# Up-projections as seven block products in 18 of 22 units of a two-layer encoder step

## The chip, the cores and the metric

One core of a Trainium2 chip. The metric is the device time of one execution in microseconds, the median of the runs shown. The engines are named as in the profile: PE (TensorE, matmuls), PEld (its weight loads), DVE (VectorE), ACT (ScalarE), POOL (GpSimd), SP (SyncE, which here only issues DMAs). Each engine works through its own queue of instructions in order; an instruction that waits holds up all that stand behind it on that engine.

## What is computed

The reference is one inference step of a two-layer trunk on 640 tokens: 512 of a new prompt and 16 next tokens of each of 8 running streams. Layer 0 has a mixer of gated spatial and convolutional heads, layer 1 a forgetting attention; each is followed by a channel mixer, the part that the change is about:

```python
def _conv_ffn(x, prev, w_up, conv_w, w_down):
    z, st = _causal_dwconv(x @ w_up, conv_w, prev)
    gate, up = jnp.split(z, 2, axis=-1)
    return (jax.nn.silu(gate) * up) @ w_down, st
```

Its input is the RMS-normed residual, d_model is 1024, d_ff is 2816, so `w_up` is 1024 x 5632 and `w_down` 2816 x 1024. All is float32. The last two rows of `x @ w_up` of each sequence are returned as new state.

## The kernel before

Tokens lie along the free axis, features on partitions. d_model is 8 chunks of 128 (`NC`), d_ff is 22 units of 128 (`NJ`), and a unit is a gate block and an up block (44 blocks, `NB`).

A float32 product is made of three float32r matmuls (`mm`): weight high times operand high, weight high times operand low, weight low times operand high. Each runs over 320 of the 640 tokens (`HT`), so one 128 x 128 piece of a weight costs six matmuls. The two halves of the tokens meet at a bank border of one PSUM tile.

Weights come from DRAM as float32 by a DMA that SP issues (`weights`); ACT casts them to the high part `whi` (L88) and DVE subtracts that from the raw tile to get the low part `wlo` (L89). The pool `wts` has three buffers of each of raw, high and low. The operands, residual times the norm's gain, are made in `prep` (ACT's `hh` L131, DVE's `hl` L132); the norm's root, one factor per token, is spread over partitions as `rb` and multiplied in when a block leaves PSUM. ACT squares the residual (L138) and POOL sums the squares (L139) for the next norm.

`ffn` treats the units in parts of 6, 6, 5 and 5. `up(j)` loads the two blocks' weights, runs 2 x 48 matmuls (`blocks`, L109), evacuates each block into a padded tile `zp` (L190 prompt, L191 streams, DVE), saves the new state (L202, POOL), convolves (one ACT product L196, two DVE taps L198 a block), applies silu to the gate (L355, ACT), multiplies gate and up (L358 and L359, DVE) and splits the product into high and low (ACT L97, DVE L98). After each part `project` runs the down-projection of that part, eight blocks, each added to the residual (L209); the next part's first unit is computed ahead of it. In the last part of layer 0 `prep` of the next norm follows each block.

The instructions of each engine are put into an order when the program is built, which need not be the order of the code: what the tables of rows below show is what stands in each engine's queue.

Of the kernel before, what the change touches and what calls it, by code (L numbers as in the profile page):

```python
# [8 lines left out]
F32 = mybir.dt.float32  # L9
# [34 lines left out]
# columns of the constants of the attention  # L44
# [4 lines left out]
NS = 256 + 16      # keys of a stream  # L49


class Core:
    def __init__(self, ctx, tc, io):
# [16 lines left out]
        self.n = 0  # L70

# [4 lines left out]
    # ---- weights: float32 from DRAM, split exactly into two float32r parts  # L76
    def weights(self, src, cols=1024, pieces=1, between=None):
        nc = self.nc
        raw = self.wp.tile([P, 1024], F32, tag="raw", name=self.nm("raw"))
# [12 lines left out]
    def split(self, pool, tags, src):  # L92
        """float32 [128, 640] -> (hi, lo) float32r tiles"""
        nc = self.nc
        hi = pool.tile([P, T], F32R, tag=tags[0], name=self.nm("sh"))
        lo = pool.tile([P, T], F32R, tag=tags[1], name=self.nm("sl"))
        nc.scalar.copy(out=hi, in_=src)  # L97
        nc.vector.tensor_tensor(out=lo, in0=src, in1=hi.bitcast(F32), op=ALU.subtract)  # L98
        return hi, lo

    # ---- products, weights stationary, tokens moving
# [10 lines left out]
    def psum(self):  # L112
        return self.pm.tile([P, 1024], F32, tag="mm", name=self.nm("mm"))
# [11 lines left out]
    # ---- RMS norm: operands scaled by g now, by the root later  # L125
# [28 lines left out]
    def stats(self, acc, pool, aux):  # L154
        """1/rms for each token, as columns [128, 5]"""
# [8 lines left out]
    def spread(self, rt, pool, aux):  # L164
        """columns [128, 5] -> the same along the free axis of every partition"""
# [727 lines left out]
```

## Time and profile before

| | |
|---|---|
| runs, us | 1533.40, 1533.43, 1536.4; median 1533.43 |
| span of the profiled execution, us | 1531.9 |
| first mixer, us from the start of the span | 0 to 227 |
| channel mixer of layer 0 | 227 to 680 |
| attention with its projections | 680 to 1076 |
| channel mixer of layer 1 | 1076 to 1523 |
| bytes moved by DMA | 142.90 MB, mean 93 GB/s |

The profiled execution's own time is its span and the little that lies around it, so that a sum of durations is made against 1531.9 us and then brought to the median of the runs. In the rows of the profile, "L109" is line 109 of the kernel; `out<-in` names tiles; after "x" stands the number of instructions; then busy time in all, mean ns of one, and the idle time of that engine ahead of them with what ended it. In rows of a timeline the first numbers are the start and the duration. In rows that group instructions by line, three numbers with slashes are the shortest, the median and the longest duration in ns. In rows by window the engines stand in the order PE, PEld, DVE, ACT, POOL, then the granted clock, the DMA share and GB/s.

### The profile page before, as it was taken

How to read it: one execution, taken by the hardware profiler on the slowest of the kernel's cores; microseconds unless marked ns; L12 is line 12 of the kernel's file. 1: busy time of each engine (PE TensorE's matmuls, PEld its weight loads, DVE VectorE, ACT ScalarE, POOL GpSimd, SP SyncE). 2: the span in 40 equal slices, each digit the busy share in tenths (PEclk: the TensorE clock that was granted, in tenths of full speed). 3: DMA queues.
4: the chain of work that ended last, by engine and by line, in shares of the span. 5: the costliest groups of instructions: out<-in, count | busy, mean ns of one | idle time of the engine just before them, and what ended most of it. 6: DMA issues, size and time to landing. Idle time of an engine off the chain costs nothing.

```text
span 1531.9 us, 26648 instructions
## 1 busy us (share of the span) xinstructions
PE 1517.8 (99%) x11008; PEld 1473.5 (96%) x11008; DVE 899.1 (59%) x1541; ACT 559.4 (37%) x918; POOL 237.4 (15%) x281
## 2 busy tenths in 40 slices
PE   8999999999999999999999999999999999999999
PEld 6999999999999999999989888888999999999998
DVE  6545437644653655675676766768765466365463
ACT  5422334322322322345545454535432233133231
POOL 5000122201210201143111111003221021021010
PEclk9999999999999999999999999999999999999999
DMA  6222212222223222243544343523222222321313
GB/s 226 77 82 73 77 56 85 68 81 85 62 64 95 64 66 93 62 156 103 180 128 136 122 123 104 183 60 107 83 60 76 87 67 57 98 73 53 107 47 106
DMA packets 52296, 142.90 MB, mean 93 GB/s; under 512 B 6656, under 2 KB 13744, under 8 KB 52048
## 3 DMA queue, kind: packets, MB, share of 16 engines
q1 hardware_dynamic: 45424, 133.79, 28.6%
q10 hardware_dynamic: 6752, 7.41, 1.4%
q8 instruction: 87, 1.43, 0.4%
q14 instruction: 33, 0.27, 0.1%
HBM read 125.41 MB, written 11.54 MB: 89 GB/s over the span
## 4 chain that ended last, share of the span: by engine, by line
PE 96%; DVE 2%; issue 1%; ACT 1%; DMA 0%; POOL 0%; SPq 0%; DVEq 0%; ACTq 0%
PE mm L109 71%; PE pj L507 10%; PE pv L583 3%; PE po L109 2%; PE pt L576 1%; PE mm L239 1%; PE pt L662 1%; PE sc L569 1%; DVE hl L132 1%; PE sc L570 1%; DVE wlo L89 1%; PE scs L641 1%; PE pt L537 1%; PE pt L655 0%; PE scs L634 0%
## 5 line engine op out<-in xcount | busy, mean ns | idle before, releaser
L88 ACT CAST whi<-raw 128x1024 fp32r<-128x1024 f32 (+4 forms) x222 | 207.6, 937 | 494.6 <-PE mm L109 426.1
L109 PE MATMUL mm<-hl,whi 128*128 128x320 f32 x1664 | 379.4, 309 | 0.5 <-DVE hl L132 0.5
L109 PE MATMUL mm<-hh,whi 128*128 128x320 f32 x1664 | 379.8, 309 | 0.0
L109 PE MATMUL mm<-hh,wlo 128*128 128x320 f32 x1664 | 379.2, 309 | 0.0
L109 PEld LDWEIGHTS mm<-hl,whi 128*128 128x128 f32 x1664 | 278.2, 188 | 0.7 <-DVE hl L132 0.7
L109 PEld LDWEIGHTS mm<-hh,whi 128*128 128x128 f32 x1664 | 278.2, 188 | 0.1
L109 PEld LDWEIGHTS mm<-hh,wlo 128*128 128x128 f32 x1664 | 278.0, 188 | 0.0
L89 DVE TENSOR_TENSOR wlo<-raw,whi 128x1024 fp32r<-128x1024 f32 (+4 forms) x222 | 245.5, 1107 | 33.3 <-ACT whi L88 33.0
L109 PE MATMUL mm<-sh,wlo 128*128 128x320 f32 x866 | 197.2, 309 | 1.3 <-DVE wlo L89 1.3
L109 PE MATMUL mm<-sl,whi 128*128 128x320 f32 x866 | 197.2, 309 | 0.0
L109 PE MATMUL mm<-sh,whi 128*128 128x320 f32 x866 | 196.2, 309 | 0.0
L202 POOL COPY so<-zp 128x18 f32<-128x18 f32 x88 | 89.4, 1016 | 570.4 <-DVE zp L191 570.4
L190 DVE TENSOR_TENSOR zp<-mm,rb 128x512 f32<-128x512 f32 x88 | 60.9, 692 | 195.8 <-PE mm L109 195.8
L209 DVE TENSOR_TENSOR x<-mm,x 128x640 f32<-128x640 f32 x79 | 65.0, 823 | 185.6 <-PE mm L109 185.6
L198 DVE SCALAR_TENSOR_TENSOR t<-zp,cst,t 128x656 f32<-128x656 f32 x184 | 165.1, 900 | 10.3 <-ACT t L196 5.6
L109 PEld LDWEIGHTS mm<-sh,wlo 128*128 128x128 f32 x866 | 144.6, 188 | 1.6 <-DVE wlo L89 1.6
L109 PEld LDWEIGHTS mm<-sl,whi 128*128 128x128 f32 x866 | 144.8, 188 | 0.0
L109 PEld LDWEIGHTS mm<-sh,whi 128*128 128x128 f32 x866 | 144.4, 188 | 0.2 <-issue 0.2
L507 PE MATMUL pj<-wlo,hh 128*128 128x256 f32 x480 | 137.7, 287 | 0.7 <-DVE wlo L89 0.7
L507 PE MATMUL pj<-whi,hh 128*128 128x256 f32 x480 | 137.7, 287 | 0.0
L507 PE MATMUL pj<-whi,hl 128*128 128x256 f32 x480 | 137.5, 287 | 0.0
L507 PEld LDWEIGHTS pj<-wlo,hh 128*128 128x128 f32 x480 | 91.6, 191 | 2.8 <-issue 1.6
(188 smaller groups left out, 1691.3 us busy)
## 6 DMA issues: line engine op xcount, KB each, us to landing
raw<-w_up SPq DMA_DIRECT2D x88, 512.0 KB
raw<-w_dn SPq DMA_DIRECT2D x32, 384.0 KB
raw<-w_c SPq DMA_DIRECT2D x24, 512.0 KB
raw<-w_dn SPq DMA_DIRECT2D x32, 320.0 KB
raw<-w_ab SPq DMA_DIRECT2D x16, 512.0 KB
ck<-c_k SPq DMA_DIRECT2D x16, 512.0 KB
cv<-c_v SPq DMA_DIRECT2D x16, 512.0 KB
o_kv<-z ACTq DMA_DIRECT2D x8, 640.0 KB
```

The lines of the kernel that those rows point to most:

```text
L88: nc.scalar.copy(out=hi[:, c], in_=raw[:, c])
L89: nc.vector.tensor_tensor(out=lo[:, c], in0=raw[:, c], in1=hi[:, c].bitcast(F32), op=ALU.subtract)
L109: nc.tensor.matmul(outs[h], lhsT=l, rhs=r[:, h * HT:(h + 1) * HT], start=start and k == 0, stop=stop and k == 2)
L132: nc.vector.scalar_tensor_tensor(out=lo, in0=x, scalar=gs, in1=hi.bitcast(F32), op0=ALU.mult, op1=ALU.subtract)
L190: nc.vector.tensor_tensor(out=op, in0=a[:, 0:TP], in1=b[:, 0:TP], op=ALU.mult)
L198: nc.vector.scalar_tensor_tensor(out=cv[:, 0:CW], in0=zp[:, i:i + CW], scalar=w[:, i:i + 1], in1=cv[:, 0:CW], op0=ALU.mult, op1=ALU.add)
L202: self.nc.gpsimd.tensor_copy(out=out.rearrange("p (s c) -> p s c", c=2), in_=zp[:, 496:ZW].rearrange("p (s c) -> p s c", c=18)[:, :, 16:18])
L209: self.nc.vector.tensor_tensor(out=x, in0=ps[:, C0:C0 + T], in1=x, op=ALU.add)
L239: nc.tensor.matmul(pvs[tb], lhsT=l[:, tb * P:(tb + 1) * P], rhs=r[:, (kc % 2) * 512:(kc % 2 + 1) * 512], start=kc == 0 and k == 0, stop=kc ...
L507: nc.tensor.matmul(out[tb], lhsT=l[:, tb * P:(tb + 1) * P], rhs=r[:, c:c + 256], start=kc == 0 and i == 0, stop=kc == 7 and i == 2)
L537: nc.tensor.transpose(t[:, tb * P:(tb + 1) * P], z[i][:, tb, pair * P:(pair + 1) * P], k.ident)
L583: nc.tensor.matmul(ov[64 * hh:64 * hh + 64, i * P:n], lhsT=z[2][:, j, (2 * pair + hh) * 64:(2 * pair + hh) * 64 + 64], rhs=u[:, j * P:(j + ...
```

## The change

In each channel mixer units 0 to 3 stay full products (`NSTD`); units 4 to 21 are computed by seven block products in the manner of Strassen and Winograd. The 2 x 2 blocks on the weights' side are (gate, up) by (even chunks, odd chunks) of d_model, and on the operands' side (even, odd chunks) by (first, second 320 tokens). A block product (`product`) is 4 chunks x 3 matmuls of 320 columns, so a unit takes 7 x 12 = 84 matmuls where it took 96.

The operand side is the same for all units. `forms(p)` makes it for chunk pair p behind each of the four full units: two DVE products of residual, gain and `rb` (640 columns), four sums or differences of 320 columns, of which three lie side by side in a raw tile, and a split of those 960 columns (ACT cast, DVE subtraction). `settle` splits the two 640-column operands into the tiles that held `hh` and `hl`, ahead of unit 4.

The weight side is made per unit (`pair_weights`): two raw tiles, four in-place sums of 512 columns on DVE, and splits of 1024, 512, 1024 and 1024 columns on ACT and DVE. `pair_blocks` runs the seven products, with ACT taking three intermediate sums out of PSUM (`snap`) and DVE and ACT writing the padded tiles; the norm's root is in the operands already. Two blocks of the down-projection of the previous part (four units) stand between the products. Their weights (`weights_down`) come two blocks to a tile; the low part is a negated copy of the high one by ACT, to which a DMA issued by GpSimd adds the weights from DRAM. Units 2 and 3 get their weights in that way as well (`weights_added`), unit 1 by `weights`. Convolutions are as before, the up block's first. Parts are now five of 4 units and one of 2; only the last one's down-projection is run by `project`. New states are copied by ACT. The host lays out the rows of `w_up` with the even chunks first (`KORD`). The pool `wts` has five buffers of high and low and four of raw; the scratch tiles in the channel mixers are 4 (9 before), the padded tiles 3 (4 before). PSUM has the same room as before, in two tiles `zx` and one `d`.

```diff
-PARTS = ((0, 6), (6, 12), (12, 17), (17, 22))
+PARTS = ((0, 4), (4, 8), (8, 12), (12, 16), (16, 20), (20, 22))
+NSTD = 4
+KORD = (0, 2, 4, 6, 1, 3, 5, 7)
...
-        self.wp = pool(ctx, "wts", bufs=3)
+        self.wp = pool(ctx, "wts", bufs=5)
...
+    def raw(self):
+        return self.wp.tile([P, 1024], F32, tag="raw", name=self.nm("raw"), bufs=4)
...
+    def added(self, pool, tags, raw, src, n, cols):
+        nc = self.nc
+        hi, lo = (pool.tile([P, n], F32R, tag=t, name=self.nm(t)) for t in tags)
+        nc.scalar.copy(out=hi[:, 0:cols], in_=raw)
+        nc.scalar.mul(out=lo[:, 0:cols], in_=hi[:, 0:cols].bitcast(F32), mul=-1.0)
+        nc.gpsimd.dma_start(out=lo[:, 0:cols], in_=src, accum_op=ALU.add)
+        return hi, lo
+    def weights_added(self, src):
+        raw = self.raw()
+        self.nc.sync.dma_start(out=raw, in_=src)
+        return self.added(self.wp, ("whi", "wlo"), raw, src, 1024, 1024)
...
+    def part(self, hi, lo, src):
+        nc = self.nc
         nc.scalar.copy(out=hi, in_=src)
         nc.vector.tensor_tensor(out=lo, in0=src, in1=hi.bitcast(F32), op=ALU.subtract)
...
+    def forms(self, p, x, g, rb, ring, fb):
+        nc = self.nc
+        pool, tags = ring
+        ys = [pool.tile([P, T], F32, tag=t, name=self.nm("y")) for t in tags]
+        tt, stt = nc.vector.tensor_tensor, nc.vector.scalar_tensor_tensor
+        for c, y in zip((2 * p, 2 * p + 1), ys):
+            stt(out=y, in0=x[c], scalar=self.gv[:, 8 * g + c:8 * g + c + 1], in1=rb, op0=ALU.mult, op1=ALU.mult)
+        (a1, b1), (a2, b2) = ((y[:, 0:HT], y[:, HT:T]) for y in ys)
+        t = self.raw()[:, 0:3 * HT]
+        t2, t3, t4 = (t[:, i * HT:(i + 1) * HT] for i in range(3))
+        tt(out=t3, in0=b2, in1=b1, op=ALU.subtract)
+        tt(out=b1, in0=a1, in1=b1, op=ALU.subtract)
+        stt(out=t2, in0=b2, scalar=-1.0, in1=b1, op0=ALU.mult, op1=ALU.subtract)
+        stt(out=t4, in0=t2, scalar=-1.0, in1=a2, op0=ALU.mult, op1=ALU.subtract)
+        return ys, self.split(fb, ("fbh", "fbl"), t, 3 * HT)
+    def settle(self, p, h, form):
+        ys, fb = form
+        for y, (hi, lo) in zip(ys, h):
+            self.part(hi, lo, y)
+        pick = lambda t, i: (t[0][:, i * HT:(i + 1) * HT], t[1][:, i * HT:(i + 1) * HT])
+        return dict(y1a=pick(h[0], 0), t1=pick(h[0], 1), y2a=pick(h[1], 0), y2b=pick(h[1], 1),
+                    t2=pick(fb, 0), t3=pick(fb, 1), t4=pick(fb, 2))
+    def pair_weights(self, gate, up):
+        nc = self.nc
+        H = 512
+        g, u = self.raw(), self.raw()
+        nc.sync.dma_start(out=g, in_=gate)
+        nc.sync.dma_start(out=u, in_=up)
+        w = ("whi", "wlo")
+        (g1, g2), (u1, u2) = ((t[:, 0:H], t[:, H:2 * H]) for t in (g, u))
+        add = lambda out, a, b: nc.vector.tensor_tensor(out=out, in0=a, in1=b, op=ALU.add)
+        A = self.split(self.wp, w, g, 1024)
+        yield
+        D = self.split(self.fd, ("dh", "dl"), u2, H)
+        add(u2, u1, u2)
+        add(u1, u1, g1)
+        B = self.split(self.wp, w, u, 1024)
+        add(g1, u2, g1)
+        add(g2, g2, g1)
+        C = self.split(self.wp, w, g, 1024)
+        pick = lambda t, i: (t[0][:, i * H:(i + 1) * H], t[1][:, i * H:(i + 1) * H])
+        yield dict(x11=pick(A, 0), x12=pick(A, 1), s3=pick(B, 0), s1=pick(B, 1), s2=pick(C, 0), s4=pick(C, 1), x22=D)
+    def product(self, out, w, f, name, start):
+        nc = self.nc
+        wh, wl = w
+        for p in range(4):
+            yh, yl = f[p][name]
+            c = slice(p * P, (p + 1) * P)
+            for i, (l, r) in enumerate(((wh, yh), (wh, yl), (wl, yh))):
+                nc.tensor.matmul(out, lhsT=l[:, c], rhs=r, start=start and p == 0 and i == 0,
+                                 stop=p == 3 and i == 2, skip_group_check=True)
+    def pair_blocks(self, w, f, zg, zu, states, downs):
+        nc = self.nc
+        zx = self.pz.tile([P, 1024], F32, tag="zx", name=self.nm("zx"))
+        Z, X = zx[:, C0:512], zx[:, 512:512 + HT]
+        Y = self.aux()[:, 0:HT]
+        n = TP - HT
+        str_ = lambda z: z[:, 514:ZW].rearrange("p (s c) -> p s c", c=18)
+        v = lambda t: t[:, n:HT].rearrange("p (s c) -> p s c", c=16)
+        def snap(b, mul):
+            t = self.fx.tile([P, HT], F32, tag="sn", name=self.nm("sn"), bufs=3)
+            nc.scalar.mul(out=t, in_=b, mul=mul)
+            return t
+        for z, st in zip((zg, zu), states):
+            nc.gpsimd.tensor_copy(out=str_(z)[:, :, 0:2], in_=st.rearrange("p (s c) -> p s c", c=2))
+        self.product(X, w["x11"], f, "y1a", True)
+        p1 = snap(X, 1.0)
+        self.product(Z, w["x12"], f, "y2a", True)
+        nc.vector.tensor_tensor(out=zg[:, 2:2 + HT], in0=Z, in1=p1, op=ALU.add)
+        self.product(Y, w["s3"], f, "t3", True)
+        p7 = snap(Y, -1.0)
+        self.product(X, w["s2"], f, "t2", False)
+        u = snap(X, -1.0)
+        if downs:
+            downs.pop(0)()
+        self.product(X, w["s1"], f, "t1", False)
+        nc.vector.tensor_tensor(out=zu[:, 2 + HT:514], in0=p7[:, 0:n], in1=X[:, 0:n], op=ALU.subtract)
+        nc.vector.tensor_tensor(out=str_(zu)[:, :, 2:18], in0=v(p7), in1=v(X), op=ALU.subtract)
+        self.product(Y, w["x22"], f, "t4", False)
+        nc.vector.tensor_tensor(out=zu[:, 2:2 + HT], in0=u, in1=Y, op=ALU.subtract)
+        if downs:
+            downs.pop(0)()
+        self.product(X, w["s4"], f, "y2b", False)
+        nc.scalar.copy(out=zg[:, 2 + HT:514], in_=X[:, 0:n])
+        nc.scalar.copy(out=str_(zg)[:, :, 2:18], in_=v(X))
+        while downs:
+            downs.pop(0)()
...
+        self.turn = (self.turn + 1) % 3
+        return self.psum_z() if self.turn < 2 else self.psum_d()
...
+        def down(n, acts, ob, w):
+            a, b = PARTS[n]
+            ps = self.psum_d()
+            for kc in range(b - a):
+                self.mm((ps[:, C0:512], ps[:, 512:512 + HT]), w, kc, acts[kc], kc == 0, kc == b - a - 1)
+            self.add_x(x[ob], ps)
+        def downs(n, acts, ob):
+            a, b = PARTS[n]
+            w = self.weights_down(io["w_dn"][l, ob:ob + 2][:, :, a * P:b * P], (b - a) * P)
+            return [lambda i=i: down(n, acts, ob + i, w[i]) for i in range(2)]
+        forms, f, prev = [], None, None
+        hk = [h[c] for c in KORD]
+        first = [KORD.index(c) for c in range(NC)]
+        zi = 0
+        for n, (a, b) in enumerate(PARTS):
+            si = self.fx.tile([P, 2, 64], F32, tag="si", name=self.nm("si"), bufs=2)
+            so = self.fx.tile([P, 2, 72], F32, tag="so", name=self.nm("so"), bufs=2)
+            nc.scalar.dma_start(out=si[:, :, 0:16 * (b - a)], in_=two(io["st_f"][l], NB)[:, :, 16 * a:16 * b])
+            acts, left = [], [0, 2, 4, 6] if n else []
+            for j in range(a, b):
+                zg, zu = self.zp[zi % 3], self.zp[(zi + 1) % 3]
+                zi += 2
+                sts = [si[:, i, 16 * (j - a):16 * (j - a) + 16] for i in range(2)]
+                if j < NSTD:
+                    blocks = (j, NJ + j)
+                    if j == 0:
+                        ps = self.blocks([self.weights(io["w_up"][l, i]) for i in blocks], hk, first)
+                    else:
+                        weights = self.weights if j == 1 else self.weights_added
+                        ps = [self.blocks([weights(io["w_up"][l, i])], hk)[0] for i in blocks]
+                    for z, p_, st in zip((zg, zu), ps, sts):
+                        self.pad_evac(z, p_[:, C0:C0 + T], rb, st)
                 else:
+                    w = self.pair_weights(io["w_up"][l, j], io["w_up"][l, NJ + j])
+                    next(w)
+                    dn = downs(n - 1, prev, left.pop(0))
+                    w = next(w)
+                    if f is None:
+                        f = [self.settle(p, (h[2 * p], h[2 * p + 1]), forms[p]) for p in range(4)]
+                    self.pair_blocks(w, f, zg, zu, sts, dn)
+                for i, z in enumerate((zg, zu)):
+                    self.new_state(z, so[:, i, 18 * (j - a):18 * (j - a) + 18])
+                acts.append(act(zg, zu, j))
+                if j < NSTD:
+                    forms.append(self.forms(j, x, g, rb, ring, fb))
+            for ob in left:
+                for d in downs(n - 1, prev, ob):
+                    d()
+            nc.scalar.dma_start(out=two(io["o_sf"][l], NB)[:, :, 18 * a:18 * b], in_=so[:, :, 0:18 * (b - a)])
+            prev = acts
+        self.project([io["w_dn"][l, ob][:, a * P:b * P] for ob in range(8)], prev, None, x, finish, cols=(b - a) * P, out=out)
```

Three places show what stands in the queues. In the rows a number behind a name is the tile's own, so one that returns is the same tile.

First, ACT's queue in layer 0 from the end of the first mixer to the end of unit 0. Before (`whi_2131` and `whi_2137` are the weights of unit 1, `whi_2265` the gate's of unit 2; `t_2110` and `t_2119` are unit 0's convolutions, `sh_2126` its product):

```order
L88 CAST whi_2131<-raw_2130 128x1024
L131 ACTIVATE hh_1956<-x_81,gv 128x640
L138 ACTIVATE t_1960<-x_81 128x640
L175 COPY rb_1973<-aux_1980 128x512
L176 COPY rb_1973<-aux_1981 128x128
L88 CAST whi_2137<-raw_2136 128x1024
L88 CAST whi_2265<-raw_2264 128x1024
L196 ACTIVATE t_2110<-zp_88,cst 128x656
L196 ACTIVATE t_2119<-zp_90,cst 128x656
L355 ACT_TABLE_LOAD
L355 ACTIVATE t_2110<-t_2110 128x656
L88 CAST whi_2271<-raw_2270 128x1024
```

After (`so_2004` are the new states, `t_2124` and `t_2128` unit 0's convolutions, `sh_2136` its product, `raw_2144` the sums of the forms; `whi_2154` and `whi_2209` are the weights of unit 1):

```order
L352 COPY so_2004<-zp_88 128x18
L352 COPY so_2004<-zp_89 128x18
L346 ACTIVATE t_2124<-zp_89,cst 128x656
L346 ACTIVATE t_2128<-zp_88,cst 128x656
L495 ACT_TABLE_LOAD
L495 ACTIVATE t_2128<-t_2128 128x656
L135 CAST sh_2136<-t_2133 128x640
L135 CAST sh_2149<-raw_2144 128x960
L94 CAST whi_2154<-raw_2153 128x1024
L94 CAST whi_2209<-raw_2208 128x1024
```

The casts of unit 1's weights stood ahead of unit 0's convolutions and now stand behind its product and its forms. The same rows follow units 1 and 2, with two negated copies behind the casts.

Second, PE's queue at the same place, the end of unit 0 and the start of unit 1. Before:

```order
L109 MATMUL mm_2009<-hh_1956,whi_2003 128x320 x2
L109 MATMUL mm_2009<-hl_1957,whi_2003 128x320 x2
L109 MATMUL mm_2009<-hh_1956,wlo_2004 128x320 x2
L109 MATMUL mm_2142<-hh_1572,whi_2131 128x320 x2
L109 MATMUL mm_2142<-hl_1573,whi_2131 128x320 x2
L109 MATMUL mm_2142<-hh_1572,wlo_2132 128x320 x2
L109 MATMUL mm_2142<-hh_1578,whi_2131 128x320 x2
```

After (`mm_2018` and `mm_2019` are unit 0's two blocks, `mm_2159` and `mm_2214` unit 1's):

```order
L251 MATMUL mm_2018<-hh_1957,wlo_2008 128x320 x2
L251 MATMUL mm_2019<-hh_1957,whi_2013 128x320 x2
L251 MATMUL mm_2019<-hl_1958,whi_2013 128x320 x2
L251 MATMUL mm_2019<-hh_1957,wlo_2014 128x320 x2
L251 MATMUL mm_2159<-hh_1573,whi_2154 128x320 x2
L251 MATMUL mm_2159<-hl_1574,whi_2154 128x320 x2
L251 MATMUL mm_2214<-hh_1573,whi_2209 128x320 x2
L251 MATMUL mm_2214<-hl_1574,whi_2209 128x320 x2
L251 MATMUL mm_2159<-hh_1573,wlo_2155 128x320 x2
L251 MATMUL mm_2159<-hh_1642,whi_2154 128x320 x2
```

In both, unit 1 follows unit 0 directly and nothing else stands between; the first matmul of unit 1 needs `whi_2154`, the fifth row needs `wlo_2155`.

Third, DVE's queue at the start of unit 4 in layer 0. Before (`wlo_2540` is unit 4's up weight, `wlo_2668` unit 5's gate weight; the evacuation of `mm_2459` is that of unit 3's up block):

```order
L89 TENSOR_TENSOR wlo_2540<-raw_2538,whi_2539 128x1024
L198 SCALAR_TENSOR_TENSOR t_2512<-zp_89,cst,t_2512 128x656 x2
L190 TENSOR_TENSOR zp_91<-mm_2459,rb_1973 128x512
L191 TENSOR_TENSOR zp_91<-mm_2459,rb_1973 128x8x16
L89 TENSOR_TENSOR wlo_2668<-raw_2666,whi_2667 128x1024
L198 SCALAR_TENSOR_TENSOR t_2521<-zp_91,cst,t_2521 128x656 x2
L358 TENSOR_TENSOR t_2525<-t_2512,t_2521 128x512
L359 TENSOR_TENSOR t_2525<-t_2512,t_2521 128x128
L98 TENSOR_TENSOR sl_2529<-t_2525,sh_2528 128x640
```

After (`raw_2589` holds the sums of the last forms, `hl_1895` is a settled operand, `raw_2602` and `raw_2603` the gate and up weights of unit 4):

```order
L158 SCALAR_TENSOR_TENSOR raw_2589<-y_2586,y_2585 128x320
L136 TENSOR_TENSOR hl_1895<-y_2585,hh_1894 128x640
L159 SCALAR_TENSOR_TENSOR raw_2589<-raw_2589,y_2586 128x320
L136 TENSOR_TENSOR sl_2607<-raw_2602,sh_2606 128x1024
L136 TENSOR_TENSOR sl_2595<-raw_2589,sh_2594 128x960
L136 TENSOR_TENSOR sl_2618<-raw_2603,sh_2617 128x512
L180 TENSOR_TENSOR raw_2603<-raw_2603 128x512
L180 TENSOR_TENSOR raw_2603<-raw_2603,raw_2602 128x512
L180 TENSOR_TENSOR raw_2602<-raw_2603,raw_2602 128x512
L180 TENSOR_TENSOR raw_2602<-raw_2602 128x512
L136 TENSOR_TENSOR sl_2624<-raw_2603,sh_2623 128x1024
L136 TENSOR_TENSOR sl_2630<-raw_2602,sh_2629 128x1024
```

Unit 4's weights were split ahead of unit 3's convolutions; now their splits and sums stand behind unit 3's forms and the settled operands.

More of the change, by code (lines that the diff above doesn't have):

```diff
@@ new lines, in weights_added, with weights_down @@
+    def weights_added(self, src):
+        raw = self.raw()
+        self.nc.sync.dma_start(out=raw, in_=src)
+        return self.added(self.wp, ("whi", "wlo"), raw, src, 1024, 1024)
+    def weights_down(self, src, n):
+        raw = self.raw()
+        hi, lo = (self.wp.tile([P, 1024], F32R, tag=t, name=self.nm(t)) for t in ("whi", "wlo"))
+        nc, m = self.nc, 2 * n
+        src = src.rearrange("o p c -> p o c")
+        two = lambda t: t[:, 0:m].rearrange("p (o c) -> p o c", o=2)
+        nc.sync.dma_start(out=two(raw), in_=src)
+        nc.scalar.copy(out=hi[:, 0:m], in_=raw[:, 0:m])
+        nc.scalar.mul(out=lo[:, 0:m], in_=hi[:, 0:m].bitcast(F32), mul=-1.0)
+        nc.gpsimd.dma_start(out=two(lo), in_=src, accum_op=ALU.add)
+        return [(hi[:, i * n:(i + 1) * n], lo[:, i * n:(i + 1) * n]) for i in range(2)]
@@ L166, in spread @@
         nc = self.nc
-        rb = pool.tile([P, T], F32, tag="rb", name=self.nm("rb"))
+        rb = pool.tile([P, T], F32, tag="acc", name=self.nm("rb"))
         dg = self.tmp()
@@ L201, in new_state @@
     def new_state(self, zp, out):
[L202 to L203 removed]
+        self.nc.scalar.copy(out=out.rearrange("p (s c) -> p s c", c=2),
+                            in_=zp[:, 496:ZW].rearrange("p (s c) -> p s c", c=18)[:, :, 16:18])
     def conv_compact(self, cv):
@@ new lines, in ffn, with act @@
+        two = lambda a, n: a.rearrange("p (u c) -> p u c", u=2)
+        def act(zg, zu, b):
+            cvs = []
+            for z, i in ((zu, 1), (zg, 0)):
+                o = O_CF + (l * NB + b + i * NJ) * 3
+                cv = self.conv(z, self.cst[:, o:o + 3])
+                if i == 0:
+                    nc.scalar.activation(out=cv[:, 0:CW], in_=cv[:, 0:CW], func=AF.Silu)
+                cvs.append(self.conv_compact(cv))
+            pr = self.tmp()
+            nc.vector.tensor_tensor(out=pr[:, 0:TP], in0=cvs[1][0], in1=cvs[0][0], op=ALU.mult)
+            nc.vector.tensor_tensor(out=pr[:, TP:T].rearrange("p (s c) -> p s c", c=16), in0=cvs[1][1], in1=cvs[0][1], op=ALU.mult)
+            return self.split(rpool, rtags, pr[:, :T])
```

94 lines of the change are left out of this document (36 added, 58 removed).

## The prediction

> **What bounds the kernel now.** I read the page's head and its chain by engine first, then what TensorE (PE) waits for, then the chain piece by piece.
>
> ```profile
> span 1531.9 us, 26648 instructions
> PE 1517.8 (99%) x11008; PEld 1473.5 (96%) x11008; DVE 899.1 (59%) x1541; ACT 559.4 (37%) x918; POOL 237.4 (15%) x281
> PE 96%; DVE 2%; issue 1%; ACT 1%; DMA 0%; POOL 0%; SPq 0%; DVEq 0%; ACTq 0%
> PE mm L239 <- ACT hh L131: 5.7, 1, 5.7
> PE mm L239 <- DVE wlo L89: 1.6, 1, 1.6
> PE mm L109 <- DVE wlo L89: 1.3, 1, 1.3
> ...
> 227.19 452.76 PE mm L109 x3087
> ...
> 1076.18 447.33 PE mm L109 x3050
> ```
>
> PE is busy 99% of the span. The third row says that 96% of the chain that ended last is PE. The waits (total, times, longest) are small and single, nearly all in the first 40 us. The two channel mixers are the last rows: 452.76 and 447.33 us without one break. So every matmul taken out there is worth its whole time, 452.76 / 3087 = 0.1467 us, as long as PE stays fed; and every microsecond in which it isn't fed is lost in full.
>
> ```profile
> 227.00:676.00 449.00, 449.00 (x3064) 449.00 (x3063) 259.63 (x353) 149.47 (x178) 71.22 (x89) 1.00 0.27 81
> ```
>
> Over layer 0's channel mixer VectorE (DVE, third busy time) works 259.63 of 449 us, ScalarE (ACT) 149.47, at a granted clock of 1.00. The helpers have room on average, so the question is where they stand in their queues when PE needs them.
>
> **What is taken out.** Up-projections of a layer: before 44 blocks x 8 chunks x 6 matmuls = 2112; after 4 units x 2 x 48 + 18 units x 84 = 1896. That is 216 fewer a layer, 432 in all: 432 x 0.1467 = **-63.4 us**. The down-projections have as many matmuls as before. This gain pays for 63.4 / 8 = 7.9 us at each of the eight hand-overs considered next (behind each full unit, four in each layer).
>
> **The hand-overs.** Before, the weight casts of the next units stand in ACT's queue ahead of the activation work of the unit just finished, and the waits above show that PE never stood there. After the change ACT's queue has the next unit's two casts behind all of it: state copies, convolutions, silu, product cast and the cast of the 960 operand columns. These wait on a DVE chain that starts with the unit's last matmul. PE has nothing else queued but the next unit, so the length of that chain is PE's idle time. Durations:
>
> ```profile
> L198 DVE SCALAR_TENSOR_TENSOR t<-zp,cst,t 128x656 f32<-128x656 f32 x88 | 78.9, 900 | 3.7 <-ACT t L196 1.5
> L89 DVE TENSOR_TENSOR wlo<-raw,whi 128x1024 fp32r<-128x1024 f32 x41 | 50.0, 1219 | 0.0
> L190 DVE TENSOR_TENSOR zp<-mm,rb 128x512 f32<-128x512 f32 x42 | 29.1, 692 | 95.5 <-PE mm L109 95.5
> L209 DVE TENSOR_TENSOR x<-mm,x 128x640 f32<-128x640 f32 x31 | 25.5, 823 | 70.9 <-PE mm L109 70.9
> L98 DVE TENSOR_TENSOR sl<-t,sh 128x640 fp32r<-128x640 f32 x22 | 18.1, 825 | 16.7 <-ACT sh L97 16.7
> L358 DVE TENSOR_TENSOR t<-t,t 128x512 f32<-128x512 f32 x22 | 15.3, 693 | 0.8
> L191 DVE TENSOR_TENSOR zp<-mm,rb 128x128 f32<-128x128 f32 x42 | 11.8, 282 | 0.0
> L359 DVE TENSOR_TENSOR t<-t,t 128x128 f32<-128x128 f32 x22 | 6.3, 285 | 0.0
> L88 ACT CAST whi<-raw 128x1024 fp32r<-128x1024 f32 x41 | 43.1, 1052 | 101.3 <-PE mm L109 98.0 <-issue 3.3
> L196 ACT ACTIVATE t<-zp,cst 128x656 f32<-128x656 f32 x42 | 35.5, 846 | 13.9 <-DVE zp L191 13.9
> L355 ACT ACTIVATE t<-t 128x656 f32<-128x656 f32 x22 | 16.6, 752 | 43.8 <-DVE t L198 43.8
> L97 ACT CAST sh<-t 128x640 fp32r<-128x640 f32 x22 | 16.0, 727 | 60.4 <-DVE t L359 60.4
> 227.48 0.27 ACT L176 COPY rb<-aux 128x128 f32<-128x128 f32 x1
> 232.50 3.33 DVE L198 SCALAR_TENSOR_TENSOR t<-zp,cst,t 128x656 f32<-128x656 f32 x4
> L774 DVE TENSOR_TENSOR x<-po,x x16: 473/491/492, 969.4 to 1031.1; 128x320 f32<-128x320 f32 x16
> ```
>
> *Behind unit 0*, from its last matmul on (0.2 us for its end to be seen): evacuation 0.61 + 0.28 (the rows' 0.69 and 0.28, overlapping a little) to 1.1; a state copy, priced by the 128-column copy's 0.27, to 1.4; convolution on ACT 0.85 to 2.2; four taps 3.33 to 5.5; silu 0.75 to 6.3; two products, 0.9 since they overlap, to 7.2. Then the forms: two 640-column operands and the split's subtraction (nearest row L98, 0.82; together 2.5, overlapping) and four of 320 columns (2.1, nearest row L774's 0.49) to 11.9. Then ACT's 960-column cast 1.0 to 12.9 and the two weight casts 1.05 each to 14.9. PE does 4 matmuls (0.6 us) in between, so it stands **14.3 us**. Weight lows, which only follow the casts, cost little more.
>
> *Behind units 1 and 2* the same chain, and then ACT's negated copies to 15.9 and an accumulating DMA for the lows, while PE gets through 8 matmuls: 14.7 us and the DMA's time L from issue to landing. No row shows such a transfer. Nearest rows:
>
> ```profile
> 0.00:18.00 18.00, 10.75 (x36) 8.33 (x36) 11.53 (x9) 14.65 (x21) 9.28 (x14) 1.00 0.88 335
> 2.58 4.82 DMA x<-xT
> ```
>
> 512 KB at the 335 GB/s of the first 18 us is 1.57 us, the low bound; a 320 KB load of x took 4.82 us in that crowd, scaled to 512 KB 7.7, the high bound. I take 4 between them, because the queues are nearly empty here (DMA share 0.27) but the landing has a fixed part. So 18.7 us each. The Trainium skill, "DMA: Bandwidth & Descriptors", section on the anatomy of one DMA, gives a GpSimd-issued transfer about 2.0 us plus its bytes at 436 GB/s, 3.2 us here; by that, an estimate, the sum would be 3 us lower.
>
> *Behind unit 3* DVE has eight subtractions of settled operands mixed into the chain, then the first pair unit's splits and sums: evacuation to 1.7, taps to 6.1, products 7.8, forms and subtractions to 13.8, then five splits (1.2, 1.1, 0.7, 1.2, 1.2) around four sums of 0.69, to 21.9. PE takes its first products at 16.5, 18.9 and 22.2, with 40 matmuls (5.9 us) in between: 22.2 - 5.9 = **16.3 us**.
>
> A layer: 14.3 + 2 x 18.7 + 16.3 = 68; two layers: **+136 us**.
>
> **The pair units.** One has 84 + 48 matmuls = 19.4 us of PE. DVE: splits 3 x 1.22 + 0.69, sums 4 x 0.69, taps 4 x 0.9, evacuations about 1.6, products 0.98, split 0.83, two residual additions 1.65: 16.0 us. ACT, by its rows, about 11.6. Neither is the bound, but the unit has two tight places: the second weight tile's cast waits for a slot that the previous unit's last down block frees, and the third product needs its low part soon after. The row of a cast (1.05) and a subtraction (1.22) against the PE work that stands there leave 0.35 to 0.5 us uncovered. I take 0.5 x 36 units = **+18 us**, bounds 0 and 1.5 each (0 to 54).
>
> **The tail and the clock.** The last part, two units deep, has 12 matmuls (1.76 us) a block, and in layer 0 the norm's preparation behind each block goes through a POOL addition:
>
> ```profile
> L132 DVE SCALAR_TENSOR_TENSOR hl<-x,gv,hh x32: 873/884/2210, 5.7 to 1067.4; 128x640 fp32r<-128x640 f32 x32
> L139 POOL TENSOR_TENSOR acc<-acc,t x28: 1572/1829/2536, 9.0 to 1066.3; 128x640 f32<-128x640 f32 x28
> ```
>
> POOL's 1.83 us is longer than 1.76, and DVE's 0.88 next to it stretches to 2.21: **+5 us**, 0 to 10.
>
> New here are long pauses of PE. The only one that the trace shows is the program's start:
>
> ```profile
> 10.11 0.61 PE L239 MATMUL mm<-whi,hh 128*128 128x512 f32 x1
> 10.54 0.41 PE L239 MATMUL mm<-whi,hl 128*128 128x512 f32 x1
> 10.79 0.40 PE L239 MATMUL mm<-wlo,hh 128*128 128x512 f32 x1
> 11.03 0.40 PE L239 MATMUL aux<-whi,hl 128*128 128x512 f32 x1
> ```
>
> The first matmul took 0.43 us to the next start, later ones 0.25 and 0.24: at most 0.4 us for each of eight pauses, **+3 us**.
>
> **Sum**: 1531.9 - 63.4 + 136 + 18 + 5 + 3 = 1630.5 us of span. The runs shown (1533.4 to 1536.4, median 1533.4) lie 1.5 us above the profiled span, so **1632 us**.
>
> **Rivals.** *Pair units bound by hand-offs.* If DVE's 16.0 us stretch beside POOL and the casts, as the 0.88 of L132 stretched to 2.21, each unit loses 1.5 to 2 us instead of 0.5: 1632 - 18 + 54 to 72 = 1668 to 1686. For: three engines hand one tile on within a product of 1.76 us. Against: DVE has 3.4 us of room. Chance 0.14.
>
> *Slow accumulating transfers.* With L of 8 to 12 us, four hand-overs cost 16 to 32 more: 1648 to 1664. For: they read and write, and start on POOL, whose queue is in order. Against: the load row's 7.7 was taken in a crowd of DMA share 0.88. Chance 0.08.
>
> *A clock that comes back slowly.* If the start's first pace, 0.43 us where 0.245 follows, lasted through the first 16 matmuls behind each pause (a third of a block), that would cost 8 x 16 x 0.1467 x 0.185 / 0.245 = 14 us: 1632 - 3 + 14 = 1643. For: no pause of PE in this trace is as long as those to come. Against: the start's slow pace holds for one matmul only, and PE had stood 10 us. Chance 0.08. The Trainium skill, "TensorE: Matmul & The Clock Gate", Part 1, puts TensorE at half clock after about 3.4 us without work, until it has worked about as long, and so speaks against a change that makes PE pause; by it, an estimate, eight pauses cost about 8 x 1.7 = 14 us too.
>
> *Faster: the hand-overs stay covered.* If the next unit's casts do get ahead of the forms' chain, as they did before the change, the 136 us go, and with them the clock's 3: 1632 - 139 = 1493. It decides at 7.9 us a hand-over, less the pair units' and the tail's 23 / 8 = 2.9, so at about 5 us. For: the whole of the trace, where PE waits for nothing at this place. Against: the order of ACT's queue, where the casts stand last, and no engine passes an instruction that waits. Chance 0.06, of which 0.01 ends within 0.2% of before.
>
> **How the numbers follow.** Forecast 0.64, the rivals 0.14, 0.08, 0.08 and 0.06. The lower end takes every unknown low: no hand-off losses (-18), L 1.57 (-10), no tail and no clock (-8), half a microsecond less at each of eight stops (-4): 1592. The upper takes 1.5 us a pair unit (+36) and L 7.7 (+15): 1683, rounded to 1685 for the tail. About 0.2% (3 us) is what a measurement of this kernel can tell from no change. Faster 0.05, within 0.2% 0.01, slower 0.94.
>
> **What the profile will show.** If right: eight stretches of 14 to 19 us without PE, behind units 0 to 3 of each layer, released by ACT's weight casts, by DVE's lows or by the DMA into wlo; 432 fewer 320-column matmuls at 0.147 us; a pair unit each 19.9 us; accumulating transfers that land in about 4 us; DVE under 85% in the pair units. Wrong if those stretches are under 5 us, if PE waits between the products of every pair unit for more than 1 us in all, if the transfers take over 8 us, or if matmuls behind a pause run at twice 0.147 us for microseconds.

## The result and the profile after

| | median, us | lowest to highest | ratio to before |
|---|---|---|---|
| before | 1533.5 | 1533.4 to 1536.4 | |
| after | 1644.0 | 1642.5 to 1646.3 | 1.0717 [1.0702, 1.0733] |

The changed kernel is 110 us slower, near the forecast of 1632 and inside its range. It came there by the hand-overs that the prediction put first, and by two other terms that were both wrong, in opposite directions; that these two nearly cancel is luck.

The head of the page, the row of the granted clock over 40 slices and the chain by engine:

```profile
span 1642.6 us, 26334 instructions
PE 1485.1 (90%) x10576; PEld 1431.1 (87%) x10576; DVE 1055.4 (64%) x1805; ACT 740.1 (45%) x1326; POOL 207.8 (13%) x235
PEclk9999986779999999999999999998767999999999
PE 86%; DVE 7%; DMA 2%; ACT 2%; issue 2%; POOL 0%; SPq 0%; DVEq 0%; ACTq 0%; POOLq 0%
```

PE has 432 instructions fewer (11008 before) and is busy 90% of the span instead of 99%. The clock row has two dents, at the start of each channel mixer; before it had none. What PE waited for (total, times, longest):

```profile
PE mm L251 <- ACT whi L102: 54.1, 4, 13.5
PE mm L251 <- ACT whi L94: 27.1, 2, 13.5
PE mm L251 <- DMA wlo<-w_up: 26.2, 4, 7.7
PE zx L201 <- ACT sh L135: 25.8, 2, 12.9
...
PE pj L690 <- DVE hl L282: 3.1, 4, 1.4
PE mm L251 <- DMA wlo<-w_dn: 2.0, 1, 2.0
PE zx L201 <- DVE sl L136: 1.6, 2, 0.8
```

These are the eight hand-overs: six first casts of a full unit's weights, four landings of accumulating transfers, two first casts of a pair unit. With the two small rows at the end they come to 54.1 + 27.1 + 26.2 + 25.8 + 2.0 + 1.6 = 136.8 us. Before, no row of this kind existed in the channel mixers. The pause behind unit 0 of layer 0, the first and the last of the forms on DVE, and then ACT (start, duration):

```profile
236.11 0.88 DVE L152 SCALAR_TENSOR_TENSOR y<-x,gv,rb 128x640 f32<-128x640 f32 x1
...
240.22 0.49 DVE L159 SCALAR_TENSOR_TENSOR raw<-raw,y 128x320 f32<-128x320 f32 x1
```

```profile
236.23 0.72 ACT L135 CAST sh<-t 128x640 fp32r<-128x640 f32 x1 [0.96 <-DVE t L499]
240.75 0.99 ACT L135 CAST sh<-raw 128x960 fp32r<-128x960 f32 x1 [3.79 <-DVE raw L159]
241.64 1.99 ACT L94 CAST whi<-raw 128x1024 fp32r<-128x1024 f32 x2
```

ACT stands idle 3.79 us for the last of the forms, although the weights behind it in its queue landed long before (SP issues no weight transfer between 205 and 242.96 us). PE on the other side of it:

```profile
228.75 0.46 PE L251 MATMUL mm<-hh,wlo 128*128 128x320 f32 x2
242.74 0.90 PE L251 MATMUL mm<-hh,whi 128*128 128x320 f32 x2 [13.53 <-ACT whi L94]
243.44 0.73 PE L251 MATMUL mm<-hl,whi 128*128 128x320 f32 x2
243.97 0.73 PE L251 MATMUL mm<-hh,whi 128*128 128x320 f32 x2
...
248.24 0.53 PE L251 MATMUL mm<-hh,wlo 128*128 128x320 f32 x2
248.60 0.46 PE L251 MATMUL mm<-hh,whi 128*128 128x320 f32 x2
```

The second thing to see is the pace behind the pause: pairs start 0.53 us apart (0.267 a matmul) until 248.2, and 0.29 or 0.30 (0.147) from 248.60 on. The start of this unit runs at little more than half pace for 5.5 us. In the pair units there is nothing of either. The first row is the window of unit 1, the second one of pair units (window, PE, PEld, DVE, ACT, POOL, granted clock, DMA share, GB/s):

```profile
242.80:259.70 16.90, 16.82 (x96) 16.56 (x96) 3.33 (x6) 1.04 (x2) 0.00 (x0) 0.83 0.20 63
...
445.00:710.00 265.00, 264.96 (x1808) 264.70 (x1808) 195.67 (x282) 140.89 (x230) 27.32 (x39) 1.00 0.43 105
```

Unit 1, 96 matmuls, takes 16.9 us at a mean granted clock of 0.83 where 14.1 would do. From 445 to 710 us PE is busy all through at 1.00, with DVE at 74%.

### The profile page after: what moved, and what is told of

Read it like the earlier page. It is cut to its first block, busy times and chain, and to the rows that moved or that the text cites. A ratio compares the mean times of both kernels' runs of the same rounds, so it can differ in the third digit from the quotient of the medians.

```text
span 1642.6 us, 26334 instructions
## 1 busy us (share of the span) xinstructions
PE 1485.1 (90%) x10576; PEld 1431.1 (87%) x10576; DVE 1055.4 (64%) x1805; ACT 740.1 (45%) x1326; POOL 207.8 (13%) x235
## 4 chain that ended last, share of the span: by engine, by line
PE 86%; DVE 7%; DMA 2%; ACT 2%; issue 2%; POOL 0%; SPq 0%; DVEq 0%; ACTq 0%; POOLq 0%
PE mm L251 36%; PE zx L201 19%; PE pj L690 10%; PE aux L201 8%; PE po L251 2%; PE pv L766 2%; DMA wlo<-w_up 2%; DVE t L348 2%; PE pt L759 1%; DVE hl L282 1%; PE mm L389 1%; DVE wlo L95 1%; PE pt L845 1%; PE sc L752 1%; DVE y L152 1%
## 5 line engine op out<-in xcount | busy, mean ns | idle before, releaser
L135 ACT CAST sh<-raw 128x1024 fp32r<-128x1024 f32 (+2 forms) x152 | 142.4, 944 | 204.5 <-PE zx L201 101.9
L201 PE MATMUL zx<-hh,sh 128*128 128x320 f32 x576 | 179.9, 312 | 25.8 <-ACT sh L135 25.8
L251 PE MATMUL mm<-hh,whi 128*128 128x320 f32 x512 | 125.6, 328 | 81.2 <-ACT whi L102 54.1
L136 DVE TENSOR_TENSOR sl<-raw,sh 128x1024 fp32r<-128x1024 f32 (+2 forms) x152 | 164.8, 1092 | 38.9 <-ACT sh L135 32.7
L201 PE MATMUL zx<-hh,sl 128*128 128x320 f32 x576 | 179.0, 312 | 1.6 <-DVE sl L136 1.6
L201 PE MATMUL zx<-hl,sh 128*128 128x320 f32 x576 | 179.5, 312 | 0.0
L251 PEld LDWEIGHTS mm<-hh,whi 128*128 128x128 f32 x512 | 91.9, 202 | 82.9 <-ACT whi L102 55.2
L251 PE MATMUL mm<-hh,wlo 128*128 128x320 f32 x512 | 120.5, 319 | 26.2 <-DMA wlo<-w_up 26.2
L201 PEld LDWEIGHTS zx<-hh,sh 128*128 128x128 f32 x576 | 109.9, 191 | 26.3 <-ACT sh L135 26.3
L251 PE MATMUL mm<-hl,whi 128*128 128x320 f32 x512 | 123.5, 324 | 0.3 <-DVE hl L282 0.3
```

Source lines behind the costliest of these rows:

```text
L201: nc.tensor.matmul(out, lhsT=l[:, c], rhs=r, start=start and p == 0 and i == 0, stop=p == 3 and i == 2, skip_group_check=True)
L251: nc.tensor.matmul(outs[h], lhsT=l, rhs=r[:, h * HT:(h + 1) * HT], start=start and k == 0, stop=stop and k == 2)
```

## The experiments

The theory: the next unit's casts stand behind the forms' chain on ACT, PE has nothing else, and each such pause costs a second time because the matmuls behind it run slowly. The rivals stand with each run. Ratios are to the kernel before, in runs on the same chip.

**Where the accumulating transfer goes: plain_lows.**

```diff
-                        weights = self.weights if j == 1 else self.weights_added
+                        weights = self.weights
```

> Units 2 and 3 get the low part of their weights by DVE's subtraction, as unit 1 does, in place of the accumulating transfer; nothing else changes. Theory (casts stand behind the forms' chain, and the transfer's landing adds to the pause): in the changed kernel PE waited 26.2 us for those four transfers, and each ended in a second slow start. Both go: 1644 - 26 - 4 = 1614 us, 1609 to 1620; the first part of all eight pauses stays at 13.5 us. Rival (DVE is as late as the transfer, the wait only changes its name): over 1634 us, with waits of 5 us or more for DVE's lows.

Measured: 1613.8 us, 1.0526 [1.0510, 1.0542], 30 less than the changed kernel. The waits at the hand-overs are now of one kind, for casts:

```profile
PE mm L251 <- ACT whi L94: 81.2, 6, 13.5
PE zx L201 <- ACT sh L135: 25.8, 2, 12.9
```

The casts' waits are the same to the tenth (54.1 + 27.1 before), and those for the transfer are gone. DVE's subtraction follows the casts closely enough to show no wait. The transfer itself, in the changed kernel, from issue to landing (L104, 8 transfers):

```profile
DMA to landing us min/median/max: 5.7/7.9/9.4
```

**Whether the pause slows what follows: busy_pauses.** On top of plain_lows:

```diff
                         self.pad_evac(z, p_[:, C0:C0 + T], rb, st)
+                    fill = self.aux()[:, 0:HT]
+                    for _ in range(22):
+                        nc.tensor.matmul(fill, lhsT=self.ones, rhs=zu[:, 2:2 + HT], start=True, stop=True)
```

> The kernel with plain lows, and 22 matmuls of 320 columns in plain float32 added behind each full unit, whose result nobody reads: they need the evacuated block, so they run in the pause, and PE works while it waits for the casts. Theory (a pause lets the granted clock fall, and the matmuls behind it run at 0.267 us for some 5 us): the pauses stay as long, the matmuls behind them run at 0.147 us from the first, and the time is about 8 x 2.5 = 20 us under that of the kernel with plain lows, near 1595 us, although it does more work. Rival (the slow start comes of ACT and DVE working beside PE, or of the operands): no gain against plain lows, near 1615 us, first matmuls still at 0.267 us.

Measured: 1599.6 us, 1.0434 [1.0419, 1.0450], 14 us under plain_lows by the medians, 18.5 by the profiled spans (1615.8 and 1597.3). The clock row of its page, and the same place in its timeline:

```profile
PEclk9999999999999999999999999999999999999999
```

```profile
229.92 12.08 PE L539 MATMUL aux<-zp,ones 128*128 128x320 f32 x44 [0.88 <-DVE zp L340]
242.58 0.56 PE L251 MATMUL mm<-hh,whi 128*128 128x320 f32 x2 [0.57 <-ACT whi L94]
242.98 0.46 PE L251 MATMUL mm<-hl,whi 128*128 128x320 f32 x2
```

The unit starts at the same moment as in the changed kernel (242.58 against 242.74), and now at full pace, with the clock at 1.00 from end to end. PE does 8 x 12.1 us of work that nobody needs, and the kernel is faster. ACT and DVE do the same beside it as in plain_lows, so they aren't what slowed the matmuls; PE's own idleness is.

**Whether it is the forms that hold the casts: forms_ahead.**

```diff
+                    forms.append(self.forms(j, x, g, rb, ring, fb))
                     for z, p_, st in zip((zg, zu), ps, sts):
                         self.pad_evac(z, p_[:, C0:C0 + T], rb, st)
...
-                if j < NSTD:
-                    forms.append(self.forms(j, x, g, rb, ring, fb))
```

> The forms of each full unit, which need nothing of that unit's result, are issued ahead of its evacuation; the same instructions. Theory (the casts wait because they stand behind the forms): the next unit's casts now stand behind the convolutions at most. By the rows, pauses of about 5.5, 3, 10.5 (the transfer's landing) and 5 us in a layer where 69 us were: 1644 - 90 - 12 for the clock = 1542 us, 1525 to 1560. Rival (the chain of evacuation, taps, silu and product holds the casts as well, the forms are only its last 5.7 us): 8 x 5.7 = 46 us less, 1595 us or more.

Measured: 1542.3 us, 1.0053 [1.0032, 1.0075]. The rival's 1595 is far off. The waits:

```profile
PE mm L251 <- DMA wlo<-w_up: 26.1, 4, 9.5
PE mm L251 <- ACT whi L94: 8.9, 2, 4.4
PE mm L251 <- ACT sh L135: 6.1, 3, 3.1
```

One instruction sequence moved in the queues takes 102 us off. Behind unit 0 there are 4.4 us left for the convolutions, where 5.5 were forecast; the transfers' landing stays, since their negated copies still stand behind convolutions.

**What is left if the weights go ahead too: both_ahead.** On top of forms_ahead:

```diff
+                    if j + 1 < NSTD:
+                        ws = load(j + 1)
+                    else:
+                        pw = self.pair_weights(io["w_up"][l, NSTD], io["w_up"][l, NJ + NSTD])
+                        next(pw)
                     forms.append(self.forms(j, x, g, rb, ring, fb))
```

Here `load(i)` gets the two weight tiles of full unit i in the way that the changed kernel does, and unit 4 continues `pw`.

> The forms ahead, and the weights of the next unit (for unit 4 its first split) issued ahead of the evacuation of the unit before. Theory: no pause behind units 0 and 1, 0 to 2 us behind unit 2, 8 to 10 behind unit 3, where the settled operands remain: 1644 - 118 - 24 for the clock = 1502 us, 1490 to 1515, below the kernel before, since the 432 matmuls stay away. Rival (DVE, which has 13 us of work in a full unit of 14 us, becomes the bound, so that what is taken from one pause returns in the next): over 1530 us, pauses with DVE busy all through.

Measured: 1512.1 us, 0.9864 [0.9848, 0.9881]: 1.4% under the kernel before, and the fastest here. The theory's 1502 was 10 short. The largest waits in its channel mixers:

```profile
PE mm L251 <- DMA wlo<-w_dn: 10.5, 2, 6.6
PE mm L251 <- ACT whi L120: 6.8, 2, 4.9
...
PE aux L201 <- DVE sl L136: 3.6, 1, 3.6
```

The pauses behind units 0 to 2 are gone; in their place unit 4 waits, for its down weights above all.

**Why the pair units cost nothing: four_slots and downs_by_dve.** The prediction had 18 us there.

```diff
-        self.wp = pool(ctx, "wts", bufs=5)
+        self.wp = pool(ctx, "wts", bufs=4)
```

> The changed kernel with four buffers of high and low weights instead of five. The prediction put 18 us on the pair units because the second weight tile's cast waits for a slot that the previous unit's last down block frees; the changed kernel's trace shows no wait there. Theory now (a unit fills four tiles and each is free long before its successor is due, so slots never bind): 1640 to 1655 us. Rival (the fifth buffer is what hid the wait, the tight place was seen rightly): one cast and one subtraction, 2.3 us, less what is covered, at each of 36 units, 1680 us or more, with waits of PE for splits in every pair unit.

Measured: 1678.0 us, 1.0932 [1.0917, 1.0947], 34 us over the changed kernel. My theory for this run fell: with four buffers the slots do bind. Its rival holds only in part. The fifth buffer does hide a wait, and the time nearly meets its 1680, but the sign that the rival named, waits for splits in every pair unit, is missing. The row that grew (2.0 us, once, in the changed kernel), the row of the splits, which is what it was, and the window of pair units:

```profile
PE mm L251 <- DMA wlo<-w_dn: 22.0, 18, 3.2
...
PE zx L201 <- DVE sl L136: 1.6, 2, 0.8
```

```profile
445.00:710.00 265.00, 258.14 (x1734) 256.56 (x1733) 189.45 (x274) 138.02 (x224) 35.86 (x39) 0.99 0.41 104
```

In the same 265 us 1734 matmuls were recorded instead of 1808. The chain shows what holds them: the down tile's cast begins only when a product of a pair unit ends (PE zx, at 590.46), and then come the negated copy and 5.8 us of transfer before PE can go on at 599.62.

```profile
590.48 0.78 ACT whi L120
...
592.38 0.96 ACT wlo L121
593.34 0.41 issue
593.75 5.82 DMA wlo<-w_dn
```

So four buffers bind, but not where the prediction put it. The late tile is the down tile and not the second weight tile, it follows a product and not the last down block, and its chain has a transfer in it. Some 20 of the 34 us are PE's waits for that transfer. With five buffers this chain is covered.

The other run of this pair:

```diff
-        nc.scalar.mul(out=lo[:, 0:m], in_=hi[:, 0:m].bitcast(F32), mul=-1.0)
-        nc.gpsimd.dma_start(out=two(lo), in_=src, accum_op=ALU.add)
+        nc.vector.tensor_tensor(out=lo[:, 0:m], in0=raw[:, 0:m], in1=hi[:, 0:m].bitcast(F32), op=ALU.subtract)
```

> The low parts of the down weights in the pair units come from DVE's subtraction instead of ACT's negated copy and the accumulating transfer: 1.22 us more for DVE in each pair unit, 1.05 less for ACT. Theory (DVE's work in a pair unit is 16 us against 19.4 of PE, so it has 3 us of room): 1636 to 1648 us, no new waits. Rival (DVE's hand-offs stand so close that any more work on it shows): 1.2 x 36 = 43 us more, 1680 or more.

Measured: 1640.4 us, 1.0689 [1.0675, 1.0704], 4 us under the changed kernel. Its row of the pair units, where the changed kernel's above has 195.67 us of DVE:

```profile
445.00:710.00 265.00, 264.96 (x1808) 264.65 (x1807) 209.43 (x295) 127.77 (x217) 16.69 (x25) 1.00 0.26 77
```

DVE carries 13.8 us more, and PE has not a matmul less: DVE has the room in the pair units that the prediction counted.

**What holds unit 4: settled_early, downs_later, downs_later_plain.** All three go on from both_ahead. The first:

```diff
-                    forms.append(self.forms(j, x, g, rb, ring, fb))
+                    for p in ((0, 1), (2,), (3,), ())[j]:
+                        forms.append(self.forms(p, x, g, rb, ring, fb))
+                    if j + 1 == NSTD:
+                        f = [self.settle(p, (h[2 * p], h[2 * p + 1]), forms[p]) for p in range(4)]
...
-                    dn = downs(n - 1, prev, left.pop(0))
+                    dn = [] if j == NSTD else downs(n - 1, prev, left.pop(0))
+                    if j == NSTD + 1:
+                        dn += downs(n - 1, prev, left.pop(0))
```

> Both ahead, and further: the forms of two chunk pairs with unit 0 and one each with units 1 and 2, the settled operands issued ahead of unit 3's evacuation, and unit 4 without down blocks (unit 5 has four), since the kernel with both ahead waited 17 us in all for the down weights of its first pair units. Theory: what is left of pauses is 5 to 7 us in a layer, all behind unit 3: 1498 us, 1490 to 1506. Rival (DVE is short of time over units 0 to 4, so the pause returns elsewhere with DVE busy all through): 1508 or more.

Measured: 1518.8 us, 0.9889 [0.9873, 0.9905]: not faster than both_ahead, whose interval it overlaps. The start of unit 4 in layer 1:

```profile
1115.00:1130.00 15.00, 10.14 (x62) 8.99 (x61) 15.00 (x23) 8.95 (x15) 0.00 (x0) 0.98 0.16 43
```

DVE works 15.00 of 15 us while PE does 62 matmuls where 102 fit. The second run takes only the last part of that diff (unit 4 without down blocks), the third adds the lows of units 2 and 3 by DVE.

> The kernel with both ahead, but unit 4 of each layer has no down blocks, and unit 5 has four: the 17 us that PE waited for the first down weights can't arise. Theory (DVE is short of time when unit 4 starts: settled operands, splits, sums and the taps of unit 3 come to some 10 us behind unit 3's end, whatever PE is given meanwhile): the wait only changes its name, PE stands 8 to 10 us in each layer for DVE's lows, 1505 to 1515 us. Rival (the down weights' landing is the cause): 17 us and a slow start less, 1490 to 1496.

> The same with the lows of units 2 and 3 by DVE: 4.9 us more for DVE ahead of unit 4. Theory (DVE short): up to 5 us a layer longer than the kernel with accumulating transfers, 1510 to 1525 us. Rival (DVE has room, the pause is the transfers'): within 3 us of it or below.

Measured: 1516.4 us, 0.9885 [0.9868, 0.9903], and 1518.3 us, 0.9897 [0.9882, 0.9913]. Neither comes near the rival's 1496. The window of the pause before unit 4 of layer 0 in the one and in the other:

```profile
272.00:285.00 13.00, 4.91 (x25) 4.25 (x24) 13.00 (x20) 7.67 (x11) 0.00 (x0) 0.78 0.35 95
```

```profile
272.00:285.00 13.00, 4.52 (x17) 3.34 (x15) 13.00 (x20) 4.67 (x7) 1.08 (x1) 0.67 0.25 62
```

While PE stands for 8 us, DVE works 13.00 of 13 us in both. In downs_later it was busy 41.2 of the 45 us ahead of that already, so its work on forms, settled operands and splits doesn't fit into four full units. The time of the third run doesn't decide between its theory and its rival: 1518.3 is 1.8 us above 1516.4, inside the ranges of both. Its waits speak for the theory. PE waits 0.5 us for a transfer of down weights where downs_later has 5.9, but some 24 us in all in either kernel, now for casts and lows. The second run's edit did less than I wanted of it, though: PE still waited those 5.9 us and 3.2 for the cast of down weights, since the first down block of unit 5 was put into unit 4's products again. So DVE's shortage is shown; how the roughly 12 us of a layer divide between it and the down weights stays open.

## Why the prediction was right, and where it was not

By its own steps, against the profiled spans (1531.9 to 1642.6, +110.7 us, 98.7 forecast):

| step | forecast, us | measured, us |
|---|---|---|
| 432 matmuls fewer | -63.4 | none of it lost: PE is busy 264.96 of 265 us in pair units |
| eight hand-overs | +136 | +136.8 by the waits |
| 36 pair units | +18 | 0 |
| tail | +5 | about 5 (3.1 for `hl` at the next projection, the rest at the residual's last additions) |
| clock | +3 | 25 of the 32 that remain |

*The matmuls.* Right. both_ahead shows it from the other side: with most pauses away the kernel is 21 us faster than before.

*The hand-overs.* Right in mechanism and size. In layer 0, behind unit 0 it was to be 14.3 and was 13.53; behind units 1 and 2 18.7 each, and was 13.53 + 5.39 and 13.53 + 7.09; behind unit 3 16.3, and was 12.90 + 0.80 + 2.00. plain_lows takes the transfers' part of it away, forms_ahead most of the rest. One size in it was off: the transfer was taken at 4 us between the bounds 1.57 and 7.7, and took 5.7 to 9.4, median 7.9. That didn't show, because the chain ahead of it was a little shorter than worked out, PE waits only for the first of a unit's two transfers (four waits for eight transfers), and it spent 2.5 us instead of 1.2 on the matmuls that it could do meanwhile. The Trainium skill, "DMA: Bandwidth & Descriptors", section on the anatomy of one DMA, gives about 2.0 us plus the bytes at 436 GB/s, by which an estimate is 3.2 us; it does not say whether its transfers accumulate, as these do. The measurement, 5.7 to 9.4, decides.

*The pair units.* The step that failed was "the row of a cast (1.05) and a subtraction (1.22) against the PE work that stands there leave 0.35 to 0.5 us uncovered". The PE work between was counted too short, and the buffer was mostly another. In the order in which PE's queue holds the matmuls of the changed kernel, the second weight tile's buffer had held the same tile of the unit before in 30 of 36 units, a down tile in only 4; and from the last use of the old high part to the first use of the new low part PE has at least 29 matmuls to do, 4.3 us, where cast and subtraction take 2.3. So the wait never comes, and the term is the lower of its bounds, 0. four_slots doesn't bring it back either: there the buffer is a down tile's in 26 units, the 29 matmuls become 23 (3.4 us), and the waits for splits stay at 1.6 us. What binds there is the longer chain of the down tile, which the prediction didn't have.

*The clock.* The step that failed was "at most 0.4 us for each of eight pauses". It rests on a misreading of the trace of the kernel before: the row at 10.11 us, taken for the program's first matmul, is the eleventh. These rows stand ahead of it:

```profile
5.68 1.22 PE L239 MATMUL mm<-whi,hh 128*128 128x512 f32 x2 [5.68 <-ACT hh L131]
6.70 0.63 PE L239 MATMUL aux<-whi,hh 128*128 128x512 f32 x1
...
9.69 0.63 PE L239 MATMUL mm<-wlo,hh 128*128 128x512 f32 x1
```

PE had stood 5.7 us and not 10, and then eleven matmuls started at least 0.42 us apart, from 5.68 to 10.54; only behind them come 0.25 and 0.24. So the trace did show a slow start of 4.9 us that costs about 2 us (11 x 0.185), and eight of them would have been 16 us instead of 3. The rival with a chance of 0.08 had the mechanism right (with 14 us, where 22 are counted below), and the argument against it, a slow pace for one matmul only, was this misreading. The prediction's own sign of being wrong came true as well, matmuls at about twice 0.147 us for microseconds.

In the changed kernel 12 to 28 matmuls behind each pause start 0.267 us apart instead of 0.147. Where a landing splits a pause in two there are two slow starts, the first cut off by the second wait after 8 matmuls. Counted from the starts of the matmuls this is 22 us over the eight pauses, and 3 more in a stretch at 0.83 in the attention's output projection. busy_pauses shows what it comes from: with PE at work in the pauses, 14 to 18.5 us go. Of the 7 us that are left of the 32, some 5 lie in the attention, which from its first projection to the first up-projection of layer 1 takes 391.8 us instead of 380.4 (3.1 of the difference are the waits for `hl`, 3 the slow stretch); what causes them stays open. The Trainium skill, "TensorE: Matmul & The Clock Gate", Part 1, states the half clock after an idle window, and the trace agrees in the pace (0.267 against 0.147); behind the unsplit pauses it lasted 3 to 6 us here, in most of them longer than the page's 3.4.

So 1632 came out near 1644 partly by luck: a loss that didn't come (18) stood against a clock that cost 22 more than forecast and 7 us that no term had.

## What to carry to other kernels

Where new work is added behind a unit, look at what already stands behind that point in each engine's queue: here the forms needed nothing of the unit, and only their place cost about 100 us. Price a pause of TensorE as the pause and then the slow matmuls behind it (22 us for eight pauses here), and look for the pauses in the granted clock by slices, which shows them at once. A row taken as the first of its kind has to be the first in the trace: here the eleven slow matmuls stood ahead of the rows that were read. A saving in matmuls that holds (63 us) is worth nothing until its preparation fits beside the work that is left: the sum of DVE's rows over the stage, compared with PE's, shows how little room four full units leave (from 227 to 285 us DVE works 54.2 of 58 us in downs_later).

## What the runs showed of the hardware

- After pauses of 13 us PE's 320-column matmuls start 0.267 us apart for 3 to 6 us, then 0.147 (changed kernel, plain_lows); with unneeded matmuls in the pause there is no such stretch, and the clock is 1.00 from end to end.
- A 512 KB accumulating transfer issued by GpSimd landed 5.7 to 9.4 us after its issue where two were issued together, and the down tiles' singly issued ones had a median of 5.9 us (row of the changed kernel's page: operation, count, size, us to landing):

```profile
wlo<-w_dn POOLq DMA_DIRECT2D x40, 512.0 KB, 5.9
```

- The times of two kernels with such pauses spread more than those of the kernel before: 1612.7 to 1617.6 for plain_lows and 1538.1 to 1545.1 for forms_ahead, where the kernel before has 1533.4 to 1534.3 in the same set. That the pauses cause it was not tested.
